# Plain products at the start of both half-step FFNs, in a hybrid decoder step on one core

## The chip, the cores and the metric

The kernel runs on one core of one Trainium2 chip. The time is device microseconds, the median of three runs. The engines are TensorE (PE, with its weight loads as PEld), VectorE (DVE), ScalarE (ACT), GpSimd (POOL) and SyncE (SP), whose queue issues all the DMAs.

## What is computed

512 prompt tokens and 8 sample tokens, 520 columns in all, go through one layer of width 1024, in fp32:

```python
def swiglu(x, w_gate, w_up, w_down):
    return (jax.nn.silu(x @ w_gate) * (x @ w_up)) @ w_down          # 1024 -> 2816 -> 1024

def layer(x, ...):
    x = x + 0.5 * swiglu(rmsnorm(x, norm_ffn1_w), ffn1_w_gate, ffn1_w_up, ffn1_w_down)
    mix, ... = token_mix(rmsnorm(x, norm_mix_w), ...)   # Mamba-2 scan, short conv, w_out
    x = x + mix
    x = x + 0.5 * swiglu(rmsnorm(x, norm_ffn2_w), ffn2_w_gate, ffn2_w_up, ffn2_w_down)
```

followed by a last RMSNorm. The outputs are the 520 rows and the new states.

## The kernel before

Everything lies transposed: features on the 128 partitions, the 520 tokens along the free axis, in two halves T0 and T1 of 260. x is four tiles `x0` to `x3` of two k-tiles each (a k-pair `e`).

Products of fp32 accuracy are made from three: an operand is split into `hi` (a cast on ACT, line 146) and `lo` (the rest, a subtraction on DVE, line 147), and PE adds hi·hi, hi·lo and lo·hi. The half of a weight split is `both`; `split` takes the next loaded item of the list `items`, splits one part of it into a pair of buffers of `whl` (four pairs) and, when the item is done, calls `load` for the next one (two raw buffers, one queue on SP). The order of the items is the order in which the kernel takes them, written out beforehand by `steps` and `ffn_items`.

A half step works on 11 pairs of hidden blocks. Each pair `p` has a gate (`G`) and an up (`U`) of 256 output features, and the down products (`D`) of earlier pairs are spread between them. Every gate or up is one `group` call: a product of 2 x 2 blocks by the seven-product scheme with shared sums (lines 218 to 241), so it needs sums of weight blocks (`adds`, lines 132 to 134, tile `S`) and sums of blocks of x. Its seven blocks are made of 12 matmuls each (four k-pairs, three products). The forms of x, called 0 to 6, are in `vbh`/`vbl` (three plain blocks, hi and lo) and `vth`/`vtl` (four sums), made by `variants` (lines 248 to 261) once for each k-pair, from x times the norm weight. `Gate` and `Up` evacuate the PSUM banks; the token's RMS factor `r` comes in there, and not into x, so the products don't wait for it. The pool `pst` has six banks.

At the start of the first half step, for each k-pair, x lands, `variants` makes its forms, and the squares go to two sums, on POOL (`square`) for the first two k-pairs and on ACT and POOL for the others. `factor` sums them over the partitions with a matmul by ones (line 286), and takes root and reciprocal (lines 287, 288). At the start of the second half step, the same forms are made by `nx2(d // 2)`, called after each pair of output features of the output projection in `mixer` (line 991 adds it to x). The pool for the weight sums, `c.sp`, is open within a half step alone; outside, `split` returns without doing anything on an item of kind "S".

In the mixer, the normed x is `Plain` (hi and lo, in the buffers of `vth`, `vtl`), the convolved channels `xs` lie six to a tile in the buffers of `vbh`, `vbl`, and the gated group's operands `gh`, `gl` (lines 980, 982) have tiles of their own. Instructions are put in order by a planner that goes by its own estimate of times; each engine then runs its queue in order.

## Time and profile before

| | us |
|---|---|
| median of three runs | 1185.29 (1183.92 to 1186.41) |
| the profiled execution, its own time | 1180.4 |
| its span, first to last instruction | 1178.6 |
| PE busy | 1117.5 (95%) |
| DVE busy | 897.8 (76%) |
| ACT busy | 523.5 (44%) |
| POOL busy | 227.1 (19%) |

All times of the trace are microseconds from the start of the span. In it, the first half step's matmuls run from 8.86 to about 391.6, the mixer's up to 799.6, the second half step's from 801.6. A busy PE isn't PE at its peak; the number of matmuls in a stretch tells more, since nearly all of them are 260 columns wide. The granted clock is a share of 2.4 GHz.

### The profile page before, as it was taken

Reading aid. Unit: us, or ns where it says so; the run is one execution under the profiler, and the core shown is the slowest. Engines: PE = TensorE matmul, PEld = TensorE weight load, DVE = VectorE, ACT = ScalarE, POOL = GpSimd, SP = SyncE. Lnnn points to the kernel's source line nnn. Section 1 sums busy time; section 2 is a strip of 40 time slices with the busy share of each in tenths; the row PEclk is TensorE's granted clock in tenths of the full one; section 3 lists DMA queues with packets and bytes.
Section 4 is the critical chain, followed back from the end, with each engine's and each line's share of the span. In section 5 each row is a group of like instructions: output and inputs, shape, how many; then the busy total and the mean of one; then the engine's idle time right before and its main releaser. Section 6 shows DMA issues by size and latency. Waiting matters only on the chain.

```text
span 1178.6 us, 21684 instructions
## 1 busy us (share of the span) xinstructions
PE 1117.5 (95%) x9059; PEld 1095.7 (93%) x9059; DVE 897.8 (76%) x1305; ACT 523.5 (44%) x750; POOL 227.1 (19%) x302
## 2 busy tenths in 40 slices
PE   4899999999999999998799999997999999999995
PEld 3799999999999999987799999997999999999994
DVE  8899777877766778889886677547988777786855
ACT  5555344444435576343322444323644444443442
POOL 5000000000002577566662232111000000000002
PEclk6899999999999999999799999998999999999998
DMA  5132332222333523455532322321332233322233
GB/s 182 36 108 77 113 131 81 81 85 98 110 100 103 157 83 118 141 171 171 177 126 79 95 73 95 103 90 36 108 103 98 75 103 108 112 99 101 78 95 73
DMA packets 45466, 122.97 MB, mean 104 GB/s; under 512 B 9336, under 2 KB 17432, under 8 KB 39864
## 3 DMA queue, kind: packets, MB, share of 16 engines
q1 hardware_dynamic: 45368, 121.58, 32.0%
q8 instruction: 71, 1.16, 0.4%
q14 instruction: 27, 0.22, 0.1%
HBM read 114.43 MB, written 7.14 MB: 103 GB/s over the span
## 4 chain that ended last, share of the span: by engine, by line
PE 79%; DVE 8%; POOL 5%; issue 3%; DMA 2%; ACT 2%; DVEq 0%; SPq 0%; POOLq 0%; ACTq 0%
PE pst L211 37%; PE auxt L522 21%; PE mmt L195 20%; DVE lo L147 2%; POOL up L891 1%; POOL st L892 1%; DVE r L288 1%; ACT hi L146 1%; DMA raw<-in_wu 1%; DMA out_ss<-st 1%; DMA st<-in_ssm 1%; DVE S L132 1%; DVE cv L766 1%; DVE vtl L261 0%; DVE y L604 0%
## 5 line engine op out<-in xcount | busy, mean ns | idle before, releaser
L146 ACT CAST hi<-raw 128x1024 fp32r<-128x1024 f32 (+2 forms) x212 | 185.8, 878 | 269.5 <-PE pst L211 86.3
L147 DVE TENSOR_TENSOR lo<-raw,hi 128x1024 fp32r<-128x1024 f32 (+2 forms) x212 | 220.3, 1040 | 50.0 <-ACT hi L146 47.3
L211 PE MATMUL pst<-vtl,hi 128*128 128x260 f32 x704 | 199.4, 284 | 6.8 <-DVE vtl L261 6.8
L211 PE MATMUL pst<-vth,hi 128*128 128x260 f32 x704 | 199.4, 285 | 4.2 <-ACT vth L260 3.5
L522 PE MATMUL auxt<-hh,hi 128*128 128x260 f32 x704 | 197.7, 283 | 1.1 <-DVE x L523 0.7
L522 PE MATMUL auxt<-hl,hi 128*128 128x260 f32 x704 | 197.6, 283 | 0.0
L211 PE MATMUL pst<-vth,lo 128*128 128x260 f32 x704 | 196.9, 284 | 0.2 <-DVE lo L147 0.2
L522 PE MATMUL auxt<-hh,lo 128*128 128x260 f32 x704 | 194.5, 283 | 0.0
L211 PE MATMUL pst<-vbh,hi 128*128 128x260 f32 x528 | 150.6, 289 | 10.7 <-ACT hi L146 5.1
L211 PE MATMUL pst<-vbl,hi 128*128 128x260 f32 x528 | 150.0, 287 | 5.1 <-DVE vbl L258 4.0
L195 PE MATMUL mmt<-vth,hi 128*128 128x260 f32 x704 | 146.5, 288 | 0.0
L211 PE MATMUL pst<-vbh,lo 128*128 128x260 f32 x528 | 145.1, 286 | 0.5 <-DVE lo L147 0.5
L195 PE MATMUL mmt<-vtl,hi 128*128 128x260 f32 x704 | 143.4, 284 | 0.0
L195 PE MATMUL mmt<-vth,lo 128*128 128x260 f32 x704 | 142.9, 285 | 0.0
L211 PEld LDWEIGHTS pst<-vtl,hi 128*128 128x128 f32 x704 | 133.5, 190 | 7.3 <-DVE vtl L261 7.3
L270 POOL TENSOR_TENSOR acc<-x 128x520 f32<-128x520 f32 x4 | 4.2, 1053 | 698.3 <-DVE x L523 678.0
L211 PEld LDWEIGHTS pst<-vth,hi 128*128 128x128 f32 x704 | 132.7, 189 | 6.4 <-ACT vth L260 4.2
L522 PEld LDWEIGHTS auxt<-hh,hi 128*128 128x128 f32 x704 | 132.2, 188 | 2.3 <-DVE x L523 1.1
L211 PEld LDWEIGHTS pst<-vth,lo 128*128 128x128 f32 x704 | 132.3, 190 | 0.8 <-DVE lo L147 0.8
L522 PEld LDWEIGHTS auxt<-hl,hi 128*128 128x128 f32 x704 | 132.5, 188 | 0.0
L522 PEld LDWEIGHTS auxt<-hh,lo 128*128 128x128 f32 x704 | 130.8, 188 | 0.0
L146 ACT CAST hi<-S 128x1024 fp32r<-128x1024 f32 x88 | 91.2, 1050 | 75.2 <-PE pst L211 53.2
(217 smaller groups left out, 2256.9 us busy)
## 6 DMA issues: line engine op xcount, KB each, us to landing
raw<-in_wi SPq DMA_DIRECT2D x45, 512.0 KB, 3.5
raw<-in_wu SPq DMA_DIRECT2D x22, 1024.0 KB, 4.9
raw<-in_wg SPq DMA_DIRECT2D x21, 1024.0 KB, 4.8
raw<-in_wd SPq DMA_DIRECT2D x48, 384.0 KB, 3.2
raw<-in_wo SPq DMA_DIRECT2D x16, 512.0 KB, 3.8
raw<-in_wd SPq DMA_DIRECT2D x16, 256.0 KB, 2.7
st<-in_ssm SPq DMA_DIRECT2D x16, 256.0 KB, 2.7
s<-scr SPq DMA_DIRECT2D x8, 512.0 KB, 4.6
```

The costliest lines, as they stand in the source:

```text
L132: V.tensor_tensor(s[:, 1:3], r[:, 0:4:2], r[:, 3:4].broadcast_to([P, 2, 512]), op=ALU.add)
L146: self.S.copy(hi, src)
L147: self.V.tensor_tensor(lo, src, hi.bitcast(F32), op=ALU.subtract)
L195: self.PE.matmul(ps[:, h, :H2], w[:, k, :], x[:, h * H2:(h + 1) * H2], start=first and n == 0, stop=last and n == 2)
L211: self.PE.matmul(ps[:, :H2], a[:, k, :], b, start=first and k + i == 0, stop=k == n - 1 and i == 2, skip_group_check=True)
L270: self.G.tensor_tensor(acc, xt, xt, op=ALU.mult)
L288: self.V.reciprocal(r[:, hs], r[:, hs])
L522: PE.matmul(ps[:, :H2], w[:, k, :], v, start=k + n == 0, stop=k == nk - 1 and n == 2)
L766: V.scalar_tensor_tensor(cv[:, :SEQ], raw[:, k:k + SEQ], w[k], cv[:, :SEQ], op0=ALU.mult, op1=ALU.add)
L891: G.tensor_tensor(up, bb, xd.unsqueeze(2).broadcast_to([P, HB, NS]), op=ALU.mult)
L892: G.tensor_tensor(st, st, up, op=ALU.add)
```

## The change

The first gates and ups of a half step (three in the first, two in the second: `LEAD`) are no longer grouped, but plain products: `pair` takes the two halves of the weights (kind "Q", no sums) and makes 2 output tiles x 2 token halves x 8 k-tiles x 3 matmuls, each output tile and half in a bank of its own.

The very first gate is written out: x is loaded by k-tile (the first one in two halves), and the gate's weights in four quarters, each between the k-tiles that need it; each k-tile's hi and lo parts and each quarter's are made as they land, and 12 matmuls follow for that k-tile into four banks. The squares of k-tiles 0 to 4 are POOL's, those of 5 to 7 ACT's, with the last two sums on DVE. The next two weights are loaded after x.

`Blocks` now keeps x's plain parts by k-tile (`xh`, `xl`, as `Plain` does), of which the grouped products' three plain blocks are slices; the four sums are made by `forms`, after the first gate and between the plain products, and no longer ahead of the start. In the second half step only the plain parts are made within the output projection.

Buffers move with it: four tiles of eight columns (`xh`, `xl`, `th`, `tl`) in place of four others; in the mixer the convolved channels take six columns each of `th` and `tl`, the sample step's B, C and update tiles and `rr` lie in their free columns, and `gh`, `gl` lie in `xh`, `xl`, where the mixer's x was.

```diff
+LEAD = {1: 3, 2: 2}
...
+        elif kind == "Q":
+            step = len(item) - 4
+            hi, lo = self.parts(None, (2, n * P))
+            self.both(r[:, 2 * step:2 * step + 2], hi, lo)
+            item.append(True)
+            self.ready.append((hi, lo))
+            if not step:
+                return
...
+    def pair_k(self, ps, w, m, k, x, first, last, hs=(0, 1)):
+        hi, lo = (t[:, k % 2 ^ m, k // 2 * P:(k // 2 + 1) * P] for t in w[m])
+        xh, xl = x
+        for h in hs:
+            for n, (a, b) in enumerate(((hi, xh), (hi, xl), (lo, xh))):
+                self.PE.matmul(ps[h][:, :H2], a, b[:, h * H2:(h + 1) * H2], start=first and n == 0, stop=last and n == 2)
+
+    def pair(self, x, bank, ev):
+        w = [self.take(), self.take()]
+        for m in range(2):
+            for h, ts in enumerate((T0, T1)):
+                ps = bank()
+                for k in range(KD):
+                    self.pair_k((ps, ps), w, m, k, x(k), k == 0, k == KD - 1, (h,))
+                ev.plain(m, ts, ps)
+            self.split()
+        ev.whole()
...
-    def variants(self, src, bh, bl, th, tl):
+    def forms(self, src, th, tl):
...
-        S.copy(bh[:, 0], src[:, 0, T0])
-        S.copy(bh[:, 1:].rearrange("p v n -> p (v n)"), src[:, 1])
...
-        V.tensor_tensor(bl[:, 0], src[:, 0, T0], bh[:, 0].bitcast(F32), op=ALU.subtract)
-        V.tensor_tensor(f(bl[:, 1:]), src[:, 1], f(bh[:, 1:]).bitcast(F32), op=ALU.subtract)
...
+    def parts(self, d, ts):
         c = self.c
...
+        w = c.par(self.wname, d)
+        xt, hi, lo = self.x[d // 2][:, d % 2, ts], self.xh[:, d, ts], self.xl[:, d, ts]
+        c.S.activation(hi, xt, AF.Copy, scale=w)
+        c.V.scalar_tensor_tensor(lo, xt, w, hi.bitcast(F32), op0=ALU.mult, op1=ALU.subtract)
...
+class Blocks(Plain):
+
+
+    def forms(self, e):
...
+        xw = c.tv.tile([P, 2, T], F32, tag="xw", name="xw")
         for m in range(2):
...
+            c.S.activation(xw[:, m], self.x[e][:, m], AF.Copy, scale=c.par(self.wname, 2 * e + m))
+        c.forms(xw, self.th[:, e], self.tl[:, e])
...
+    def plain(self, m, ts, ps):
+        self.c.V.tensor_tensor(self.dst[:, m, ts], ps[:, :H2], self.r[:, ts], op=ALU.mult)
...
-    for e in range(NQ):
-        for m in range(2):
-            nc.sync.dma_start(x[e][:, m], a["xT"][2 * e + m])
-        if e == 0:
-            c.load(pieces=2)
-    c.load()
...
-            if start:
-                for e in range(NQ):
-                    nx.operands(e)
-                    if e == 0:
-                        c.adds()
-                        c.split()
-                    for m in range(2):
-                        if e < 2:
-                            c.square(acc[0], x[e][:, m], e + m == 0)
-                        elif e + m == 2:
-                            S.activation(acc[1], x[e][:, m], AF.Square)
-                        else:
-                            c.square(acc[1], x[e][:, m], False, True)
...
+                raw = c.raw.tile([P, 4 * 512], F32, tag="raw", name="raw").rearrange("p (b m) -> p b m", b=4)
+                w0 = [c.parts(None, (2, 512)) for _ in range(2)]
+                ps = [(bank(), bank()) for _ in range(2)]
+                for k in range(KD):
+                    e, m = divmod(k, 2)
+                    for i, hs in enumerate((T0, T1) if k == 0 else (slice(0, T),)):
+                        nc.sync.dma_start(x[e][:, m, hs], a["xT"][k][:, hs])
+                        nx.parts(k, hs)
+                        if m == 0 and i == 0:
+                            q = slice(e * P, (e + 1) * P)
+                            nc.sync.dma_start(raw[:, :, q], a["wg1"][0][:, :, q])
+                            for j, (hi, lo) in enumerate(w0):
+                                c.both(raw[:, 2 * j:2 * j + 2, q], hi[:, :, q], lo[:, :, q])
+                    for j in range(2):
+                        c.pair_k(ps[j], w0, j, k, nx.of(k), k == 0, k == KD - 1)
+                    if k < 5:
+                        c.square(acc[0], x[e][:, m], k == 0)
+                    elif k == 5:
+                        S.activation(acc[1], x[e][:, m], AF.Square)
+                    else:
+                        sq = c.tv.tile([P, T], F32, tag="t4", name="sq2")
+                        S.activation(sq, x[e][:, m], AF.Square)
+                        V.tensor_tensor(acc[1], acc[1], sq, op=ALU.add)
+                c.load()
+                c.load()
                 c.prime()
                 r = c.factor(acc, D)
+                ev = Gate(c, fp, g, r)
+                for j in range(2):
+                    for h, ts in enumerate((T0, T1)):
+                        ev.plain(j, ts, ps[j][h])
+                ev.whole()
+                nx.forms(0)
+                nx.forms(1)
+                later = [2, 3]
             else:
                 c.prime()
                 r = nx.factor()
+                later = list(range(NQ))
...
+                if kind != "D":
+                    if kind == "G" and i[0]:
+                        while later:
+                            nx.forms(later.pop(0))
...
+                    if 2 * i[0] + (kind == "U") < LEAD[n]:
+                        c.pair(nx.of, bank, ev)
+                    else:
+                        c.group(NQ, B, bank, ev)
                 if kind == "G":
...
+                    while len(later) > 2:
+                        nx.forms(later.pop(0))
...
+        xst = [c.vp.tile([P, KD, T], F32, tag=n, name="xs") for n in ("th", "tl")]
+        rr = xst[1][:, 7]
+        place = [t[:, :SEQ].rearrange("p (b n) -> p b n", n=NS) for t in (xst[0][:, 6], xst[0][:, 7], xst[1][:, 6])]
...
-                    hi = yp.tile([P, T], F32R, tag=f"gh{j}", name=f"gh{j}")
...
+                    if j == 0:
+                        gh, gl = (c.vp.tile([P, KD, T], F32R, tag=n, name="g" + n) for n in ("xh", "xl"))
```

## Rows read from the trace of the kernel before

**Rows 1.** The page, part 1: busy us, share of the span, instructions.

```profile
PE 1117.5 (95%) x9059; PEld 1095.7 (93%) x9059; DVE 897.8 (76%) x1305; ACT 523.5 (44%) x750; POOL 227.1 (19%) x302
```

**Rows 2.** Busy time by stretch (stretch, its length, engines, clock, DMA share, GB/s).

```profile
core 0: us, PE busy (x) PEld busy (x) DVE busy (x) ACT busy (x) POOL busy (x), PEclk, DMA share, GB/s
9.00:20.00 11.00, 4.27 (x13) 2.77 (x13) 11.00 (x9) 5.34 (x8) 8.53 (x5) 0.50 0.50 201
40.00:60.00 20.00, 18.86 (x150) 18.17 (x149) 14.98 (x19) 10.52 (x15) 0.00 (x0) 1.00 0.15 54
60.00:80.00 20.00, 20.00 (x167) 19.92 (x166) 19.35 (x28) 12.00 (x17) 0.00 (x0) 1.00 0.31 106
...
200.00:260.00 60.00, 60.00 (x500) 59.79 (x499) 46.56 (x69) 25.14 (x34) 0.00 (x0) 1.00 0.31 105
...
760.00:820.00 60.00, 52.86 (x415) 51.47 (x414) 35.08 (x37) 19.60 (x29) 6.12 (x4) 0.94 0.21 71
820.00:840.00 20.00, 20.00 (x167) 19.85 (x167) 17.32 (x26) 11.93 (x18) 0.00 (x0) 1.00 0.29 106
```

**Rows 3.** The same by stretch for line 211, the grouped products' matmuls, alone.

```profile
0.00:20.00 20.00, 4.41 (x13) 2.91 (x13) 0.72 0.62 216
20.00:40.00 20.00, 9.13 (x29) 6.73 (x30) 0.59 0.15 52
40.00:60.00 20.00, 18.86 (x150) 18.17 (x149) 1.00 0.15 54
```

**Rows 4.** PE's waits (total us, times, longest), 0 to 60, then 760 to 830.

```profile
PE pst L211 <- DVE vbl L258: 4.0, 1, 4.0
...
PE pst L211 <- DVE vtl L261: 4.5, 1, 4.5
PE pst L211 <- DVE x L991: 1.8, 1, 1.8
```

**Rows 5.** Timeline of POOL and DVE at the start (start, us, instruction, wait before it).

```profile
4.00 1.05 POOL L270 TENSOR_TENSOR acc<-x 128x520 f32<-128x520 f32 x1 [3.57 <-DMA x<-in_xT]
...
9.84 1.54 POOL L276 TENSOR_TENSOR sq<-x 128x520 f32<-128x520 f32 x1 [2.09 <-DMA x<-in_xT]
...
11.45 2.15 POOL L277 TENSOR_TENSOR acc<-acc,sq 128x520 f32<-128x520 f32 x1
...
12.38 2.32 DVE L261 TENSOR_TENSOR vtl<-t,vth 128x1040 fp32r<-128x1040 f32 x1
...
35.20 1.17 DVE L261 TENSOR_TENSOR vtl<-t,vth 128x1040 fp32r<-128x1040 f32 x1
```

**Rows 6.** Timeline of PE, two matmuls in a row.

```profile
39.23 0.42 PE L211 MATMUL pst<-vth,hi 128*128 128x260 f32 x1
...
39.45 0.39 PE L211 MATMUL pst<-vtl,hi 128*128 128x260 f32 x1
```

**Rows 7.** Groups of DVE by line and shape, whole span: busy, mean ns | idle before.

```profile
L147 DVE TENSOR_TENSOR lo<-S,hi 128x1024 fp32r<-128x1024 f32 x88 | 106.7, 1220 | 16.6 <-ACT hi L146 16.5
...
L380 DVE TENSOR_TENSOR g<-cp,pst 128x260 f32<-128x260 f32 x66 | 27.8, 421 | 10.5 <-PE pst L211 6.8 <-ACT cp L366 2.9
...
L405 DVE TENSOR_TENSOR g<-g,r 128x1040 f32<-128x1040 f32 x22 | 27.2, 1237 | 2.7 <-ACT g L404 2.7
...
L288 DVE RECIPROCAL r<-r 128x260 f32<-128x260 f32 x10 | 17.2, 1750 | 2.5 <-ACT r L287 2.5
...
L403 DVE TENSOR_TENSOR g<-g,r 128x520 f32<-128x520 f32 x22 | 15.3, 695 | 0.2
...
L315 DVE SCALAR_TENSOR_TENSOR vtl<-x,pc,vth 128x520 fp32r<-128x520 f32 x8 | 6.0, 756 | 0.6 <-ACT vth L314 0.6
```

**Rows 8.** Timeline: last z product's evacuation, first gated operand's matmuls, later row sums.

```profile
707.09 0.68 DVE L962 TENSOR_TENSOR z<-mmt,r 128x520 f32<-128x520 f32 x1
...
719.00 0.40 PE L195 MATMUL mmt<-gh,hi 128*128 128x260 f32 x2
...
804.61 1.14 PE L286 MATMUL auxt<-acc,ones 128*128 128x260 f32 x4
```

**Rows 9.** Group of POOL by line and shape: the sample step's updates.

```profile
L891 POOL TENSOR_TENSOR up<-bb,xd 128x512 f32<-128x512 f32 x16 | 25.5, 1593 | 28.4 <-DVE ys L896 28.3
```

More of the change, by code (lines that the diff above doesn't have):

```diff
@@ L344, in __call__, with factor, of @@
             self.acc = c.new_acc()
-        self.operands(e)
+        for d in (2 * e, 2 * e + 1):
+            self.parts(d, slice(0, T))
+            c.square(self.acc, self.x[e][:, d % 2], d == 0, True)
+    def factor(self):
+        return self.c.factor([self.acc], D)
+    def of(self, k):
+        return self.xh[:, k], self.xl[:, k]
+class Blocks(Plain):
+    def forms(self, e):
+        c = self.c
+        if e == 0:
+            self.th, self.tl = (c.vp.tile([P, NQ, 4, H2], F32R, tag=n, name="f" + n) for n in self.tags[2:])
+        xw = c.tv.tile([P, 2, T], F32, tag="xw", name="xw")
         for m in range(2):
-            c.square(self.acc, self.x[e][:, m], e + m == 0, True)
+            c.S.activation(xw[:, m], self.x[e][:, m], AF.Copy, scale=c.par(self.wname, 2 * e + m))
+        c.forms(xw, self.th[:, e], self.tl[:, e])
     def __getitem__(self, vk):
         v, k = vk
-        return (self.bh[:, k, v], self.bl[:, k, v]) if v < 3 else (self.th[:, k, v - 3], self.tl[:, k, v - 3])
-    def factor(self):
-        return self.c.factor([self.acc], D)
+        if v < 3:
+            d, ts = ((0, T0), (1, T0), (1, T1))[v]
+            return self.xh[:, 2 * k + d, ts], self.xl[:, 2 * k + d, ts]
+        return self.th[:, k, v - 3], self.tl[:, k, v - 3]
 class Evac:
@@ L419, in c12, with plain, whole @@
         c.V.tensor_tensor(h[:, 1], h[:, 1], g[:, 1], op=ALU.mult)
+    def plain(self, m, ts, ps):
+        self.c.V.tensor_tensor(self.dst[:, m, ts], ps[:, :H2], self.g[:, m, ts], op=ALU.mult)
+    def whole(self):
+        pass
 def steps(n):
@@ L479, in build, with ffn @@
     acc = [c.new_acc(), c.new_acc()]
-    for e in range(NQ):
-        for m in range(2):
-            nc.sync.dma_start(x[e][:, m], a["xT"][2 * e + m])
-        if e == 0:
-            c.load(pieces=2)
-    c.load()
-    def ffn(nx, start, after, halves_last=None):
+    def ffn(n, nx, after, halves_last=None):
         with ExitStack() as c2:
@@ L495, in ffn @@
             bank = lambda: pp.tile([P, 512], F32, tag="ps", name="pst")
[L496 to L508 removed]
+            g = fp.tile([P, 2, T], F32, tag="g", name="g")
@@ L573, in last @@
         if e == 0:
-            ys.append(c.vp.tile([P, KD, T], F32, tag="vth", name="y"))
+            ys.append(c.vp.tile([P, KD, T], F32, tag="th", name="y"))
             ys.append(c.new_acc())
@@ L586, in last_half @@
         PE.matmul(ps[:, :H2], c.ones, facc[:, hs], start=True, stop=False)
-        sq = c.vp.tile([P, 2, H2], F32, tag="vbl" if h else "vbh", name="sq")
+        sq = c.vp.tile([P, KD, T], F32, tag="xl" if h else "xh", name="sq")[:, :2, :H2]
         S.activation(sq, x[e][:, :, hs], AF.Square)
@@ L607, in last_half @@
                 nc.sync.dma_start(o["yT"][:, e0:e1, ts], y[:, e0:e1, ts])
-    ffn(nx2, False, last, last_half)
+    ffn(2, nx2, last, last_half)
 def mixer(c, o, x, nxt, nx2):
@@ L753, in mixer @@
         xs = [None] * NX
-        xst = [c.vp.tile([P, 6, T], F32, tag=n, name="xs") for n in ("vbh", "vbl")]
         def conv(i):
@@ L870, in sample @@
             HB = NB // 2
-            bcs = sd.tile([P, HB, NS], F32, tag="up", name="bcs")[:NB]
+            bcs = place[2][:NB]
             V.tensor_copy(bcs.rearrange("b t n -> b (t n)"), pbc[:NB])
@@ L877, in sample @@
                     bs = slice(k * HB, (k + 1) * HB)
-                    bb = sd.tile([P, HB, NS], F32, tag="bb", name="bb")
-                    cc = sd.tile([P, HB, NS], F32, tag="cc", name="cc")
+                    bb = place[0]
+                    cc = place[1]
                     nc.sync.dma_start(bb, scb[g, bs].unsqueeze(0).broadcast_to([P, HB, NS]))
@@ L889, in sample @@
                             S.activation(st[:, b], st[:, b], AF.Copy, scale=ddc[:, j, 1, k * HB + b:k * HB + b + 1])
-                        up = sd.tile([P, HB, NS], F32, tag="up", name="up")
+                        up = place[2]
                         G.tensor_tensor(up, bb, xd.unsqueeze(2).broadcast_to([P, HB, NS]), op=ALU.mult)
```

70 lines of the change are left out of this document (24 added, 46 removed).

## The prediction

> **What bounds the kernel now.** I read the page's first part, then a table of busy time by stretch. The page says that TensorE (PE) is at work nearly all the time [rows 1]. The table says where it is not: in a stretch from the middle of the first half step PE is busy for the whole 60 us and issues 500 matmuls, 0.12 us each, while the stretches ahead of 60 us and the one that holds the second half step's start fall short of that [rows 2]. So the kernel is PE's matmul count times 0.12 us, plus what PE loses at a few places, and the change touches two of them.
>
> Start of the first half step: PE has issued only 192 of that half step's matmuls by 60.0 us [rows 3]. At 0.12 us they are 23.0 us, so 37 us were lost. PE's waits name the forms of x one after another, VectorE's (DVE's) vbl and vtl among them [rows 4]. DVE is busy through the whole of 9 to 20 us in spite of only nine instructions [rows 2]: the timeline shows why [rows 5]. A DVE instruction that took 1.17 us alone took 2.32 us with a GpSimd (POOL) one beside it, and a POOL one that took 1.05 us alone took 2.15. In that stretch the two engines take turns. Third, the granted clock is at the low level (0.50, 1.2 GHz) there, and matmuls start 0.22 us apart [rows 6].
>
> Start of the second half step: 760 to 820 us holds 415 matmuls where 500 would fit, 85 x 0.12 = 10.2 us lost, and 820 to 840 is full again [rows 2]. The waits are 4.5 us for vtl of the last k-pair and 1.8 us for the last x [rows 4]; the clock fell with them.
>
> **The change, part by part.** Durations of DVE by size [rows 7]: 128x260 0.42, 128x520 0.70, 128x520 with a scalar 0.76, 128x1024 1.22, 128x1040 1.24, a reciprocal of 128x260 1.75.
>
> *More matmuls.* A grouped gate or up is 7 blocks x 4 k-pairs x 3 = 84 matmuls; a plain one is 2 x 2 x 8 k-tiles x 3 = 96. Three in the first half step add 36, 4.3 us; two in the second add 24, 2.9 us. All on the path.
>
> *The first gate, k-tile by k-tile.* It needs of DVE, ahead of each k-tile, the low part of x (0.76; the first k-tile in two halves, 0.84) and, every other k-tile, two low parts of a weight quarter (128x256, 0.42 each by the nearest size). Through k-tile 3 this is 0.84 + 0.84 + 0.76 + 0.76 + 0.84 + 0.76 = 4.8 us. POOL squares five k-tiles with nine instructions. If the two engines take turns as they do there [rows 5], k-tile 3 is ready after 4.8 us of DVE and eight POOL instructions of 1.05: from the 4.0 us at which the first x had landed [rows 5], 4.0 + 4.8 + 8.4 = 17.2. K-tile 2 is ready one x part and one POOL turn or so earlier, at about 15.6. A k-tile is 12 matmuls: 2.6 us at the low level, 1.44 at the high one. I take two of them from 15.6 at the low level and the last four at the high one, since PE then has a queue of ready matmuls, as from 40 us on, where the clock is at 1.00 [rows 2]: 15.6 + 5.2 + 5.8 = 26.6. The DVE side of the last k-tile ends at 4.0 + 9.5 (POOL) + 10.2 (17 low parts and one sum of squares) = 23.7, so it does not set the end. Bounds: 20 if POOL costs DVE nothing, 31 if the clock stays low. Landing isn't the limit: the third x k-tile landed at 9.84 behind 1 MB of weights [rows 5], and here 0.25 MB stand ahead of it. On SP's queue 13 issues replace 10, and the next weights go behind them; the second of these loads waits there for the first gate's buffer, till its last low part at about 22, with nothing queued behind that the first gate needs, and nothing of the two is due before the first gate ends.
>
> *What stays ahead of the comparison point.* Before has 2904 - 192 = 2712 matmuls of the half step left at 60.0 us. After has 2940, so it has as many left after 228: the first gate's 96 and 132 more, 15.8 us. The four matmuls with the ones matrix for the row sums take 1.1 us [rows 8]. The gate's four banks of six come free only when the factor is there: last square about 24, row sums, two reciprocals (3.5 us), first evacuation, about 33; the first up needs its third bank 48 matmuls in, at 27.7 + 5.8 = 33.5. I put 0.5 us on it (0 to 2).
>
> *The forms of x made meanwhile.* Four calls of 0.70 + 2 x 0.42 + 1.24 = 2.8 us of DVE, 11.1 in all, now beside the plain products. First grouped product is the second up; its third block is the first to read a form, at 27.7 + 23.0 + 2.9 = 53.6. DVE has from 23.7 until then 29.9 us, and these are ahead: a sum 0.7, reciprocals 3.5, first gate's evacuation 4 x 0.42 + 1.24 = 2.9, low parts of the first up 2.4, forms 11.1, the first up's evacuation 1.7, second gate's low parts 2.4 and evacuation 1.7, the sums for the second up's weights 1.22 + 2 x 0.7 = 2.6, its first two low parts 2.4: 31.4 us. Two more of 1.24 each, the low part of h and the gate's last product, may go ahead: 33.9. So PE waits 1.5 to 4; I take 2.5 (0 if the queue order is lucky, 6 if forms come last). Dropping vbl (1.1 us of DVE per k-pair) is in this list by absence; ScalarE has room (5.34 of 11 us in the first of these stretches [rows 2]).
>
> First half step: 26.6 + 1.1 + 15.8 + 0.5 + 2.5 = 46.5 against 60.0: 13.5 us gained.
>
> *Second half step.* x's parts are two instructions per k-tile instead of the whole set, made inside the output projection, so at its end only the last evacuation (0.70), a ScalarE copy and a 0.76 us low part stand between x and its k-tile, which PE reaches after 21 matmuls (2.5 us): 0.4 us of wait. The plain weights need no sums, and so are split ahead of this start; the grouped ones couldn't be, as their pool was not open. Of the 10.2 us lost, the row sums' 1.1 stay, 0.4 too, 2.9 go to the added matmuls. For the forms the same list: due 27.4 us after the projection's end, against 0.7 + 0.76 + 1.2 + 3.5 + 2.9 + 11.1 + 1.7 + 1.24 + 2.6 + 2.4 = 28.1 of DVE, with some idle at its start: again 2.5 (0 to 6). Gain 10.2 - 1.1 - 0.4 - 2.9 - 2.5 = 3.3.
>
> *Mixer.* The gated part's operands now live where the mixer's x lay, and so are written only after the last z product: eight low parts of 0.76, 6 us, between the last z at 707.09 and their first matmul at 719.00 [rows 8]. They fit: 0 (0 to 3). The other renamed places (rr, B, C and the update in free columns) add no instruction: 0, but see the second rival.
>
> Sum: 13.5 + 3.3 = 16.8 us. The profiled execution took 1180.4 (span 1178.6); it would take 1163.6. The median of the runs is 1185.3, 4.9 above; I take the difference of 16.8 over to it and predict 1168.5.
>
> **Rivals.** *Forms late.* If both waits for forms are at their upper end, 6 us, the time is 1168.5 + 7 = 1175.5. For it: DVE is at 19.35 of 20 us in 60 to 80 us even now [rows 2]. Against: plain weights take two low parts and no sums, where grouped ones take four low parts and 2.6 us of sums. Chance 0.20.
>
> *Low clock through the first gate.* PE waits for each k-tile, the clock stays at the low level, and the gate ends at 31: 1168.5 + 4.4 = 1173. The clock is at 1.2 GHz through the stretch in which PE waits between matmuls [rows 2, 6], which speaks for it; that k-tiles 3 to 7 come about 1.6 us apart, (23.7 - 17.2) / 4, faster than PE eats them at that level (2.6), speaks against. The Trainium skill ("TensorE: Matmul & The Clock Gate", section "HAM oscillation — how this bites in real kernels") describes a kernel in which each k-tile's work was shorter than the wait for the next, so that the clock fell anew at every one; by that rule the time is this rival's. The trace agrees that the low level goes with waits. Chance 0.12.
>
> *Renamed places serialise the mixer.* B, C and the update tile now share two tiles with the convolved channels. If waits went by tile and not by column, the sample step's 16 rounds would wait for the scan's instructions and hold them back; POOL already waits 28.4 us in those rounds [rows 9], and as much again on PE's path gives 1168.5 + 28 = 1197, slower. It decides from 16.8 / 16, about 1 us a round. Against: the channels shared tiles before too, and no such wait shows. Chance 0.06.
>
> *No earlier start.* If the planner orders PE so that the first gate's matmuls wait as the grouped ones did, the first half step gains nothing and pays 4.3: 1185.3 + 4.3 - 3.3 = 1186. Chance 0.05.
>
> **How the numbers follow.** Forecast 1168.5, chance 0.57. Its bounds: gate at 20 and no waits for forms, 6.6 + 0.5 + 5 = 12 less, 1156; the upper ends of all, 1180. Together these corners are unlikely, so 8 in 10 is 1158 to 1178, which takes in the first two rivals. A measurement tells 0.2%, 2.4 us, from no change. Faster: 0.57 + 0.20 + 0.12 = 0.89, less 0.01 for the corners, 0.88; same 0.05 (most of the fourth rival, and a corner); slower 0.07.
>
> **What would show it.** First matmuls of the first gate about 6 us instead of 8.86, its last about 27; DVE and POOL lengthened beside each other until about 18; about 228 half-step matmuls issued by 46 us; 415 matmuls in the 60 us around the second start becoming about 475; a wait of PE on vtl's successor of 1.5 to 4 us at the first grouped product of each half step; the mixer's length unchanged. If the mixer changes by more than 3 us, or PE waits at the plain products for weights, the sum is wrong.

## The result, and the profile after

The changed kernel takes 1173.19 us (median of four runs, 1166.82 to 1176.91) against 1185.17 for the kernel before in the same comparison (1183.92 to 1186.41): ratio 0.9893, interval 0.9848 to 0.9938. It is faster by 12 us where 16.8 were forecast, and the forecast's 1168.5 is 4.7 us too low.

The profiled execution of the changed kernel took 1172.36, its span is 1170.6. Busy time, share and instructions, from the first part of its page, beside [rows 1]:

```profile
PE 1123.9 (96%) x9119; PEld 1101.7 (94%) x9119; DVE 871.6 (74%) x1279; ACT 514.4 (44%) x731; POOL 224.6 (19%) x301
```

PE issues exactly 60 matmuls more than before (9119 against 9059): the 36 and 24 of the sum. Then the table of busy time by stretch, which answers [rows 2] (stretch, its length, the engines, granted clock, DMA share, GB/s):

```profile
9.00:20.00 11.00, 9.12 (x54) 8.18 (x52) 10.65 (x10) 6.46 (x14) 9.59 (x7) 1.00 0.61 221
...
40.00:60.00 20.00, 19.31 (x155) 18.57 (x154) 19.00 (x30) 11.42 (x14) 0.00 (x0) 1.00 0.16 54
60.00:80.00 20.00, 18.15 (x140) 17.20 (x141) 16.06 (x23) 9.53 (x15) 0.00 (x0) 1.00 0.15 53
760.00:820.00 60.00, 58.72 (x486) 58.41 (x485) 37.76 (x44) 22.53 (x28) 7.48 (x4) 1.00 0.24 85
820.00:840.00 20.00, 15.40 (x106) 13.11 (x105) 15.38 (x22) 10.54 (x16) 0.00 (x0) 1.00 0.13 47
```

Three things are to be seen. The start works: PE issues 54 matmuls in 9 to 20 where it issued 13, at a clock of 1.00 where it had 0.50. There is a hole that was not there, from the end of 40 to 60 (155 where 167 fit) into 60 to 80 (140, where before had 167). And the hole of the second start has not gone, it has moved: 760 to 820 now lacks 14 of 500 instead of 85, but 820 to 840, which was full, lacks 61 of 167. 61 x 0.12 = 7.3 us.

The plain products' matmuls alone (line 256) up to 46.5 us, the moment that the forecast named, answer [rows 3]; the grouped products have issued none by then:

```profile
0.00:46.50 46.50, 35.98 (x257) 34.27 (x258) 1.00 0.48 161
```

PE's largest waits, first two of 0 to 60 and then three of 760 to 830 (total us, times, longest), beside [rows 4]:

```profile
PE pst L256 <- DVE lo L149: 1.7, 3, 0.7
PE pst L256 <- DVE g L427: 1.3, 1, 1.3
...
PE pst L221 <- DVE lo L149: 1.4, 2, 1.0
PE pst L256 <- DVE x L1053: 1.3, 1, 1.3
PE pst L221 <- DVE fxl L286: 0.8, 1, 0.8
```

No single wait is long any more: 1.3 us at most. In the holes PE goes on with other blocks for as long as it has some, and waits in many small pieces; there the count of matmuls in a stretch says more than the list of waits.

To place gains and losses I cut each execution at two instructions: the start of the first half step's last down matmul, and the start of the last evacuation of the mixer's output projection. For the kernel after they are the last times of these two lines (count, shortest/median/longest ns, first to last start):

```profile
L576 PE MATMUL auxt<-hh,lo x43: 278/282/283, 360.0 to 378.2; 128*128 128x260 f32 x43
...
L1053 DVE TENSOR_TENSOR x<-mmt,x x8: 686/699/700, 722.9 to 790.8; 128x520 f32<-128x520 f32 x8
```

Cut so, in us, one profiled execution in each row, with the experiments in the order in which they are told below:

| kernel | first half step ends | mixer | second half step | span |
|---|---|---|---|---|
| before | 391.4 | 409.4 | 377.8 | 1178.6 |
| before, again | 391.9 | 411.1 | 379.7 | 1182.7 |
| after | 378.2 | 412.6 | 379.8 | 1170.6 |
| after, again | 379.1 | 411.7 | 379.9 | 1170.7 |
| forms first in both half steps | 385.4 | 407.5 | 372.2 | 1165.1 |
| three plain products in the second | 378.9 | 409.7 | 375.8 | 1164.4 |
| own buffer for xw | 381.6 | 407.2 | 378.0 | 1166.8 |
| own buffer, forms first in both | 380.0 | 410.3 | 371.6 | 1161.9 |
| forms first in the second only | 379.6 | 416.7 | 372.8 | 1169.1 |
| the same, again | 378.6 | 411.5 | 372.1 | 1162.2 |
| own buffer, forms first in the second | 381.6 | 410.8 | 371.8 | 1164.2 |
| no squares on POOL | 372.3 | 414.2 | 380.7 | 1167.2 |
| squares on ACT | 381.5 | 413.0 | 372.3 | 1166.8 |
| one plain product fewer in each | 387.7 | 412.6 | 382.3 | 1182.6 |

By the means of the two executions of either kernel, the first half step gained 13.0 us (forecast 13.5), the second lost 1.1 (forecast a gain of 3.3), and the mixer is 1.9 longer (forecast 0): 10.0 in all. The medians differ by 12.0; single executions of the changed kernel lie up to 10 us apart, and where two profiles of one kernel differ by 6.9 us (forms first in the second only, below), 5.2 of it lie in the mixer. Most of what follows is on the second half step, which is 4.4 us off its forecast.

### The profile page after: what moved, and what is told of

It is laid out like the page before. It is cut to its first block, busy times and chain, and to the rows that moved or that the text cites. A ratio compares the mean times of both kernels' runs of the same rounds, so it can differ in the third digit from the quotient of the medians.

```text
span 1170.6 us, 21766 instructions
## 1 busy us (share of the span) xinstructions
PE 1123.9 (96%) x9119; PEld 1101.7 (94%) x9119; DVE 871.6 (74%) x1279; ACT 514.4 (44%) x731; POOL 224.6 (19%) x301
## 4 chain that ended last, share of the span: by engine, by line
PE 80%; DVE 6%; POOL 4%; issue 3%; DMA 3%; ACT 3%; SPq 0%; DVEq 0%; POOLq 0%; ACTq 0%
PE pst L221 32%; PE mmt L205 21%; PE auxt L576 20%; PE pst L256 3%; DVE lo L149 2%; POOL xs L955 1%; POOL st L956 1%; ACT hi L148 1%; DMA st<-in_ssm 1%; DMA raw<-in_wu 1%; DMA out_ss<-st 1%; PE auxt L904 0%; DVE y L666 0%; DVE xxl L339 0%; POOL ce L871 0%
## 5 line engine op out<-in xcount | busy, mean ns | idle before, releaser
L148 ACT CAST hi<-raw 128x1024 fp32r<-128x1024 f32 (+3 forms) x218 | 188.5, 869 | 292.8 <-PE mmt L205 105.7
L149 DVE TENSOR_TENSOR lo<-raw,hi 128x1024 fp32r<-128x1024 f32 (+3 forms) x218 | 227.0, 1044 | 60.5 <-ACT hi L148 57.6
L205 PE MATMUL mmt<-xxh,hi 128*128 128x260 f32 x704 | 146.5, 289 | 0.0
L205 PE MATMUL mmt<-xxl,hi 128*128 128x260 f32 x704 | 143.8, 285 | 0.0
L205 PE MATMUL mmt<-xxh,lo 128*128 128x260 f32 x704 | 143.6, 286 | 0.0
L205 PEld LDWEIGHTS mmt<-xxh,hi 128*128 128x128 f32 x704 | 110.2, 190 | 0.6
L205 PEld LDWEIGHTS mmt<-xxl,hi 128*128 128x128 f32 x704 | 110.0, 190 | 0.3 <-issue 0.2
L205 PEld LDWEIGHTS mmt<-xxh,lo 128*128 128x128 f32 x704 | 110.0, 191 | 0.1
L149 DVE TENSOR_TENSOR lo<-S,hi 128x1024 fp32r<-128x1024 f32 x78 | 94.4, 1218 | 19.6 <-ACT hi L148 19.3
L221 PE MATMUL pst<-fxh,hi 128*128 128x260 f32 x320 | 90.7, 286 | 0.8 <-ACT hi L148 0.4
```

Source lines behind the costliest of these rows:

```text
L148: self.S.copy(hi, src)
L149: self.V.tensor_tensor(lo, src, hi.bitcast(F32), op=ALU.subtract)
L205: self.PE.matmul(ps[:, h, :H2], w[:, k, :], x[:, h * H2:(h + 1) * H2], start=first and n == 0, stop=last and n == 2)
L221: self.PE.matmul(ps[:, :H2], a[:, k, :], b, start=first and k + i == 0, stop=k == n - 1 and i == 2, skip_group_check=True)
```

## Experiments

Theory A: the loss behind the plain products is a matter of buffers. A form's call scales x into `xw`, and `xw` has the same single buffer as `h`, the up's result; so the calls for k-pairs 2 and 3 can't begin before `h` of the first up has been read. Theory B, the prediction's: DVE has too much to do by the time the forms are due. Theory C came out of the runs: it is the place of the calls in the program. The change calls the forms of pairs 2 and 3 behind the first up.

**The changed kernel again.**

> The changed kernel once more, unaltered, for a second profile and more runs. In its first profile the first half step gained 13.3 us (its matmuls end at 378.3 instead of 391.6), the mixer took 3.3 us more (412.5 us from there to the last sum of the output projection, before 409.2), and the second half step 1.6 us more (380.4 instead of 378.8 us from the projection's last matmul to the end). If the mixer's 3.3 us come from the new order and places, they are here again, 412 to 413; if they are a matter of one execution, the mixer takes 408 to 414 and differs from the first profile by more than 1 us. Time: 1167 to 1177 either way.

1173.27 us (1171.64 to 1174.14), ratio 0.9911 (0.9896 to 0.9926). The mixer's 411.7 lies just outside the 412 to 413 of the one case and within 1 us of the first profile, which the other excluded, so it decides nothing. The second half step is again 379.9, and 55 to 75 us again holds 128 matmuls: both holes are the kernel's, not one execution's.

**All forms ahead of the first up.**

```diff
-                later = [2, 3]
+                nx.forms(2)
+                nx.forms(3)
+                later = []
...
-                    while len(later) > 2:
+                    while later:
```

> All four calls for the forms of x stand ahead of the first up instead of two ahead of it and two behind. Theory A, a buffer: the scratch tile xw, of which there is one, also holds the first up's result h, so that the last two calls wait until h's low part is made (their first instruction stands at 46.34 and 819.53 us, right behind it). Then the last form's low part ends about 10 us earlier in both half steps (before 50 and before 818), PE's lost matmuls at 55 to 75 us (38, 4.6 us) and at 820 to 840 (61, 7.3 us) mostly come back: 7 to 11 us faster than the changed kernel, about 1163. Theory B, DVE's load, as predicted: DVE has more to do ahead of the first grouped product than fits, and the order doesn't matter much: the wait moves to the first up, within 2 us of the changed kernel.

1169.96 us (1166.84 to 1172.82), ratio 0.9884 (0.9862 to 0.9906), between what the two theories gave. The small total hides two large parts: the second half step is 7.6 us shorter than after's, its hole is gone, and the first is 7.2 us longer. PE's longest wait between 25 and 60 us says why:

```profile
PE pst L256 <- DVE h L449: 7.6, 1, 7.6
```

The first up has no bank left because its result can't be written: `h` waits for the buffer, which now the last two calls' `xw` hold. So the shared buffer is a price, but a price of this order, not of the changed kernel's.

**Three plain products in the second half step too.**

```diff
-LEAD = {1: 3, 2: 2}
+LEAD = {1: 3, 2: 3}
```

> Three plain products instead of two in the second half step: the second gate is plain there too. It adds 12 matmuls, 1.4 us. The first grouped product comes 11.5 us of PE later, so that forms that end at about 830 us would be there in time. Theory A and B both give the 7.3 us lost at 820 to 840 back for 1.4: 5 to 6 us faster than the changed kernel, 1167. If the loss there isn't from the forms but from the weights' buffers (of four pairs, freed only as PE goes on), it stays, and the time is 1 to 2 us longer than the changed kernel's.

1168.46 us (1166.23 to 1170.92), ratio 0.9879 (0.9861 to 0.9897). Twelve more matmuls, 1.4 us, and yet the second half step is 4.0 us shorter. What PE lost there was waiting for forms, and plain work fills it. Both theories had expected 5 to 6 us less in all, and the medians differ by 4.7; the rival, by which the loss stays, is refuted.

**A buffer of its own for xw**, out of the ring that holds `hh`; the order of the program stays. (A buffer of its own for `h` instead, the first idea, has no room: its pool would need 40.625 KB per partition where 36.75 are left, so there is no time for it.)

```diff
+            fw = [hp.tile([P, 2, T], F32, tag="hh", name="xw") for _ in range(NQ)]
...
-        xw = c.tv.tile([P, 2, T], F32, tag="xw", name="xw")
```

> The scaled x of the forms (xw) gets a buffer out of the ring of hh tiles instead of the one buffer that it shares with the up's result h. Program order, planner and all instructions stay those of the changed kernel; the forms of pairs 2 and 3 still stand behind the first up. Theory A (the shared buffer holds the forms): the ACT copies of xw no longer wait for hl of the first up; the last low part of the forms ends some 5 to 8 us earlier than 60.5 and 828.8, the stretches 55 to 75 and 820 to 840 get back most of their 4.6 and 7.3 us, and the time falls by 7 to 11 us from the changed kernel's 1173, to 1162 to 1166. Theory B (VectorE's load holds them, as the prediction had it): the copies are earlier, but the subtractions end where they did, and the time stays within 2 us of 1173. A third case: the order that the planner gives VectorE, with the up's evacuations ahead of the forms, holds them, in which case only part comes back (2 to 5 us).

1174.2 us (1168.56 to 1175.78), ratio 0.9893 (0.9864 to 0.9923): the median did not move. Theory A falls. The second half step gained 1.8 us, the first lost 3.4. ACT's timeline (start, us, instruction, the wait before it) shows what still holds the forms, first in the kernel after, then in this one:

```profile
809.86 1.05 ACT L148 CAST hi<-S 128x1024 fp32r<-128x1024 f32 x1 [2.33 <-PE pst L256]
815.68 0.62 ACT L148 CAST hi<-raw 128x512 fp32r<-128x512 f32 x1 [4.77 <-PE pst L256]
816.21 1.06 ACT L609 CAST hh<-h 128x1040 fp32r<-128x1040 f32 x1
...
819.53 1.34 ACT L366 ACTIVATE xw<-x,pc 128x520 f32<-128x520 f32 x2
```

```profile
813.79 0.62 ACT L148 CAST hi<-raw 128x512 fp32r<-128x512 f32 x1 [4.77 <-PE pst L256]
814.32 1.07 ACT L610 CAST hh<-h 128x1040 fp32r<-128x1040 f32 x1
815.30 2.58 ACT L365 ACTIVATE xw<-x,pc 128x520 f32<-128x520 f32 x4
```

x had been there since the projection's end, about 790, and with the ring the buffers were free. But ACT stood still for 4.77 us before a weight cast that waits for the plain up's matmuls to let go of a weight buffer, and the scaling of x stands behind that cast and behind the cast of `h`. With the ring all four scalings run in one go (x4). Counted from the last evacuation's start they begin after 26.5 us instead of 28.7, and that is about what the buffer gives: 1.8 us.

**Own buffer, and all forms first.** Both edits together.

> As the run before, and the forms of all four pairs stand right behind the first gate in both half steps, ahead of the first up's evacuation. With the forms' order alone (the run forms_first) the first half step lost 7.3 us because the first up's result could not be written before the forms had let go of the shared buffer. Theory A: with a buffer of their own that loss is gone but for the up's evacuations standing behind more VectorE work (0 to 2 us); the second half step keeps the 7.6 us it gained; in all 1161 to 1165. Theory B (VectorE's load): the first half step is still about 7 us longer than in the changed kernel, since the subtractions ahead of the evacuation are the same; 1168 to 1171.

1164.75 us (1163.11 to 1165.94), ratio 0.9821 (0.9802 to 0.984). The second half step is 371.6, and 55 to 75 us holds 165 matmuls: both holes are gone. The same stretch in after and in this kernel (PE, clock, DMA share, GB/s):

```profile
55.00:75.00 20.00, 17.46 (x128) 1.00 0.20 74
```

```profile
55.00:75.00 20.00, 19.76 (x165) 1.00 0.25 81
```

The first half step still ends no earlier than after's, for another reason:

```profile
PE pst L256 <- DVE g L426: 5.2, 1, 5.2
```

That is the wait for banks ahead of the first gate's evacuation, 1.3 us in after. In this execution the first reciprocal begins at 30.64 and the first evacuation at 36.18 (26.84 and 32.43 in after). From the one to the other it is 5.5 and 5.6 us, so what is late is the reciprocal, by 3.8 us. ACT had waited 4.85 us for a load, and the last row sums, for which the root waits, come later on PE's queue, in after and in this kernel:

```profile
24.45 1.92 PE L311 MATMUL auxt<-acc,ones 128*128 128x260 f32 x8
```

```profile
29.03 1.04 PE L311 MATMUL auxt<-acc,ones 128*128 128x260 f32 x4
```

This is not one execution's: the run with one plain product fewer (below), which has the same start, has its last row sums at 29.44, ACT's wait for a load at 5.01 and the wait for banks at 4.9. With the buffers free, ACT also scales x between the first gate's k-tiles (11.00 busy of 9 to 20, against 6.46 in after). Which of these makes the factor late no run tells apart. Theory B's 7 us are not there.

**Forms first in the second half step only**, buffers as in the changed kernel; run twice.

```diff
-                    while len(later) > 2:
+                    while len(later) > (2 if n == 1 else 0):
```

> Buffers as in the changed kernel; the forms of pairs 2 and 3 stand ahead of the first up in the second half step alone, the first half step is untouched. If the two half steps' losses are independent, the second half step is some 7 us shorter (372 against 379.8) and the first stays at 378 to 379: 1164 to 1167. If the gain of forms_first in its second half step came from something that its slower first half step set up (other chance of the clock, DMA phase), it isn't seen here: 1172 to 1174.

1167.39 us (1164.48 to 1170.92), ratio 0.9836 (0.9813 to 0.9859): the two half steps are as the first case had them (379.6 and 372.8, a little over on the first), the median is 0.4 above its range.

> The run second_first once more, beside the run before on the same chip: which of the two is the better, and whether its long mixer (416.7 us from the first half step's last matmul to the last evacuation of the output projection, with the clock at 0.61 behind the wait at the mixer's start) was that execution's. If chance: first half step 378 to 380, second 372 to 373 again, mixer 407 to 413, profile 1160 to 1166, median 1165 to 1168. If the order of the second half step had a hand in the mixer: 415 to 418 again, profile 1168 to 1171.

1163.99 us (1161.57 to 1165.49), ratio 0.9815 (0.9786 to 0.9845). The second half step took 372.8 and 372.1, both times 7 us or more less than after, by order alone. This is theory C. The first run's long mixer, 416.7, was that execution's: the second has 411.5. The same stretches by 5 us (columns as above), kernel after and then the second run of this one:

```profile
805.00:810.00 5.00, 5.00 (x44) 5.00 (x43) 3.02 (x5) 2.64 (x4) 0.00 (x0) 1.00 0.01 3
...
815.00:820.00 5.00, 5.00 (x43) 5.00 (x43) 3.65 (x7) 3.33 (x5) 0.00 (x0) 1.00 0.36 123
820.00:825.00 5.00, 3.75 (x28) 3.12 (x26) 3.69 (x5) 3.31 (x6) 0.00 (x0) 1.00 0.21 87
825.00:830.00 5.00, 2.93 (x16) 2.11 (x16) 3.83 (x5) 1.87 (x2) 0.00 (x0) 1.00 0.01 2
```

```profile
805.00:810.00 5.00, 5.00 (x44) 5.00 (x43) 4.19 (x7) 4.85 (x6) 0.00 (x0) 1.00 0.01 3
...
815.00:820.00 5.00, 5.00 (x44) 5.00 (x43) 5.00 (x9) 2.99 (x5) 0.00 (x0) 1.00 0.16 26
820.00:825.00 5.00, 5.00 (x43) 5.00 (x43) 2.82 (x4) 2.10 (x4) 0.00 (x0) 1.00 0.45 188
```

In after DVE is idle for 1.98 of 805 to 810 and 1.35 of 815 to 820, while PE is about to run dry for want of DVE's results. In the other kernel it is idle for 0.81 and 0, and PE stays full. The groups of the forms' low parts tell the same (count, ns, first to last start):

```profile
L286 DVE TENSOR_TENSOR fxl<-t,fxh x4: 1234/1242/1242, 792.5 to 828.8; 128x1040 fp32r<-128x1040 f32 x4
```

```profile
L286 DVE TENSOR_TENSOR fxl<-t,fxh x4: 1228/1232/1241, 791.8 to 816.4; 128x1040 fp32r<-128x1040 f32 x4
```

From the last evacuation's start (790.8 and 790.1) the last form ends after 39.2 us in the one and 27.5 us in the other. With the forms first this is near the 28.1 us of the forecast's list of DVE's work; in the changed kernel's order it is not. The nearness is in part luck: DVE is busy for 25.4 of the 27.5 us, the low part of `h` that the list holds comes only behind, and x's last low part takes 1.80 us where the list has 0.76.

**Own buffer, forms first in the second half step only.**

> xw in a buffer of its own, the first half step's forms in the changed kernel's order (pairs 2 and 3 behind the first up), the second half step's all ahead of the first up. Theory (the order counts, the buffer only where forms go ahead of the up): the first half step ends where the changed kernel's does, 378 to 379.6, and the 381.65 of the run xw_ring was the low clock of that execution; the second half step takes 371.5 to 373; median 1164 to 1167. Rival (the buffer of its own lets forms 2 and 3 in ahead of work that is due earlier, as xw_ring's 381.65 may say): the first half step ends at 381 to 382 again, and the median is 1166 to 1169.

1165.83 us (1164.68 to 1166.34), ratio 0.9832 (0.9804 to 0.986). By the first half step the rival holds: it ends at 381.6 again, as in the first run with the buffer (the median itself lies in the theory's range). 55 to 75 us, here and in that first run (columns as in the last such rows):

```profile
55.00:75.00 20.00, 16.06 (x97) 0.83 0.15 55
```

```profile
55.00:75.00 20.00, 16.04 (x97) 0.83 0.16 59
```

97 matmuls both times, 128 in after. What I had called one execution's low clock comes with this kernel. With the buffer free, DVE's instructions fall into another order: in the earlier of these two runs the second form's low part starts at 49.8 instead of 43.3 and the last at 62.6 instead of 60.5, and PE waits 2.6 us for low parts of weights (L149). Which of these brings the clock down the runs leave open.

**No squares on POOL at the start.** The squares of k-tiles 1 to 4 and their sums are left out, so the first norm's factor lacks these terms.

```diff
-                    if k < 5:
-                        c.square(acc[0], x[e][:, m], k == 0)
+                    if k == 0:
+                        c.square(acc[0], x[e][:, m], True)
+                    elif k < 5:
+                        pass
```

> GpSimd's squares of k-tiles 1 to 4 and their sums are left out at the start (the first norm's factor then lacks these four terms, so the values after it differ). Theory: GpSimd and VectorE lengthen each other while both work on SBUF, and that paces the first gate's k-tiles; without the squares VectorE's casts of 9 to 20 us go at their later speed and the first gate's last matmul ends at 20 to 22 us instead of 24.5, and the whole is 2 to 4 us shorter. Rival: the loads pace the k-tiles; the gate ends within 0.5 us of 24.5 and the whole is unchanged.

The first half step ends at 372.3, 5.9 us earlier than after's, and the one time is 1169.01. The gate's last matmul starts at 20.57 instead of 24.34, as the theory had it. DVE's timeline in the kernel after and in this one:

```profile
13.45 3.26 DVE L339 SCALAR_TENSOR_TENSOR xxl<-x,pc,xxh 128x520 fp32r<-128x520 f32 x2
16.64 2.71 DVE L149 TENSOR_TENSOR lo<-raw,hi 128x256 fp32r<-128x256 f32 x2
```

```profile
11.08 1.43 DVE L339 SCALAR_TENSOR_TENSOR xxl<-x,pc,xxh 128x520 fp32r<-128x520 f32 x2
12.42 0.75 DVE L149 TENSOR_TENSOR lo<-raw,hi 128x256 fp32r<-128x256 f32 x2
```

Two low parts of weights take 2.71 us beside POOL's squares and 0.75 without them. The Trainium skill ("SBUF — State Buffer", section "SBUF: two separate sides") says that a VectorE instruction with two operands in SBUF and a GpSimd one that reads SBUF exclude each other for a whole instruction; the trace agrees, as far as these lengthened times (2.71 against 0.75) can show it.

**Squares on ACT instead**, on top of own buffer and forms first.

```diff
-                        c.square(acc[0], x[e][:, m], k == 0)
+                        c.square(acc[0], x[e][:, m], k == 0, True)
```

> The run xw_ring_first (own buffer for xw, all forms right behind the first gate), and beside that the squares of k-tiles 1 to 4 are taken by ScalarE instead of GpSimd, which is left with the sums of them: about half of GpSimd's work at the start. Nothing is left out. Theory (GpSimd and VectorE take turns, and that paces the first gate): half of what leaving out the squares gave in the first half step, about 3 of 6 us; the gate's matmuls end at about 22 to 23 us and the median falls from 1164.75 to 1161 to 1163. Rival: ScalarE, which the changed kernel's trace has busy for 6.00 of the 6 us from 9 to 15, becomes the pace with four more squares of 0.62 us; no gain or a loss of up to 2 us, 1164 to 1167.

1165.32 us (1162.73 to 1168.57), ratio 0.983 (0.9809 to 0.9852): no gain over 1164.75; the rival holds. 9 to 20 us, and POOL's sums with their waits:

```profile
9.00:20.00 11.00, 9.54 (x72) 8.67 (x72) 7.94 (x13) 11.00 (x22) 2.47 (x2) 1.00 0.61 222
```

```profile
20.79 1.31 POOL L302 TENSOR_TENSOR acc<-acc,sq 128x520 f32<-128x520 f32 x1 [5.21 <-ACT sq L299]
23.74 1.77 POOL L302 TENSOR_TENSOR acc<-acc,sq 128x520 f32<-128x520 f32 x1 [1.64 <-ACT sq L299]
```

DVE has room (7.94 of 11 us), PE issues 72 matmuls (54 in after, 56 in the run that it starts from). But ACT is busy for all 11, as it was in that run even without these squares (11.00), the sums come late, and the wait for the first gate's banks is 7.0 us instead of 5.2. What the gate gained the factor gave back.

**One plain product fewer in each half step**, on top of own buffer and forms first.

```diff
-LEAD = {1: 3, 2: 2}
+LEAD = {1: 2, 2: 1}
```

> The run xw_ring_first with one plain product fewer in each half step: gate and up in the first, the gate alone in the second. This shows what the plain products cover. In xw_ring_first the last forms were there at 61.3 and 818.3, and the first grouped product began at about 54 and 815.4. Theory (the forms' chain of some 5 us a pair sets when grouped products can run, and the plain products only hide it): each half step saves 12 matmuls, 1.4 us, and waits longer for the forms, by 5 to 10 us in the first and 2 to 8 us in the second; in all 5 to 15 us slower than xw_ring_first, profile 1167 to 1177. Rival (the planner has enough other blocks, or the forms come as much earlier as they are needed earlier): 1 to 3 us faster than xw_ring_first.

1184.5 us, span 1182.6: 20.7 us longer than the run that it starts from, slower than either theory said. The first half step lost 7.7 and the second 10.7; the rest, 2.3, lies in the mixer. The cover of two plain products, 192 matmuls or 23 us, is worth many times the added matmuls.

**The kernel before again.**

> The kernel before once more, for a second profile of its mixer. In the changed kernel and its variants the stretch from the first half step's last matmul to the start of the second half step's work took from 407 to 417 us, where the one profile of before has 409.2; the clock had fallen behind the wait at the mixer's start in four of eight. If the change has a hand in it (the mixer's loads come later against a first half step that ends 13 us earlier), before has its wait there at 1.4 to 1.6 us again, the clock at 1.00 behind it, and 407 to 410 us. If it is chance alone, before may show 411 to 414 and the low clock as well. One more profile can refute the first, not prove it.

1184.52 us: mixer 411.1, clock 1.00 behind the wait, and the wait itself 1.7 us. So before alone spans 409.4 to 411.1, and the twelve executions with the changed mixer 407.2 to 416.7, mean 411.5 against 410.3. That is no difference these runs can tell; neither expectation is refuted. One part of it may go with the change. PE's wait at the mixer's start, in before and in after:

```profile
PE auxt L684 <- ACT tbl L296: 1.5, 1, 1.5
```

```profile
PE auxt L749 <- ACT tbl L321: 1.9, 1, 1.9
```

Behind it stands a load: ACT's cast ahead of the norm's factor waits 0.6 us for a weight load in before, 1.0 in after, and 2.0 in the run without squares, where PE waits 2.9. PE's wait is 1.5 and 1.7 us in the two executions of before and 1.4 to 2.9, mean 2.1, in the twelve with the changed mixer; ten of these are above 1.7. It is 1.9 to 2.9 in the six in which the first half step ends at 379.6 or earlier, but 2.3 and 2.4 at 381.6 and 381.5 as well. So some 0.5 us may be given back there; that the earlier end of the first half step does it is not shown.

## Why the prediction was right or wrong

*Added matmuls: right.* 60, as counted.

*First gate: right in its mechanism, 2.0 us too long.* The first matmul starts at 5.39 (about 6 was expected), the last ends at 24.34 + 0.28 = 24.6 where 26.6 was forecast, with the turns of DVE and POOL that [rows 5] showed. I let two k-tiles run at the low clock, 2 x (2.6 - 1.44) = 2.3 us; here it was at 1.00 throughout, and in the eleven other executions of the changed kernel and its variants between 0.84 and 1.00 over 9 to 20 us (1.00 in six). So the rival of the low clock did not come about. It drew on the Trainium skill ("TensorE: Matmul & The Clock Gate", section "HAM oscillation — how this bites in real kernels"), whose kernel has each k-tile's work shorter than the wait for the next. That is not so in this trace, which thus neither bears the page out nor speaks against it: a k-tile's 12 matmuls are 1.44 us, and PE's longest single wait in the gate was 0.7. The run without squares shows that the turns set the pace: 3.8 us of the gate. (The 0.22 us between matmuls that I put to 9 to 20 us I had read at 39 us [rows 6].)

*Bank wait: 0.5 forecast, 1.3 measured*, within its bounds.

*Forms in the first half step: 2.5 forecast, 4.7 measured.* 257 matmuls were out by 46.5 us instead of 228, since the wait was not yet paid: 29 x 0.12 = 3.5 us ahead. Then 55 to 75 us held 128 instead of 167: 39 x 0.12 = 4.7. That it is the forms' place and buffer is seen from the runs in which this stretch is full (165 matmuls, above), not from a wait: no single long one is there, as the forecast had expected. The gate's 2.0 too long and the forms' 2.2 too short nearly cancel and leave 13.0 beside the 13.5. The sum was right in part by that luck, and the total does not vouch for its terms.

*Second half step: wrong, and this is the step that failed.* "For the forms the same list ... again 2.5 (0 to 6)". I had summed DVE's work and put it against the due time as if DVE could do it in any order. The sum itself was near, in part by luck: 27.5 us when the forms stand first. What failed is that in this program they stand behind the first up, on ACT's queue behind casts that wait for weight buffers (4.77 us at a stretch), so that DVE had idle time and the forms came 39.2 us in. The price was 7.3 us, outside the bounds of 0 to 6. The 0.4 us for x, put behind 21 matmuls, was 1.3 and stood elsewhere: PE waits for the last evacuation (L1053, above) ahead of its very first plain matmul, as it had for 1.8 us before. 10.2 us had been lost before; now it is (14 + 61) x 0.12 = 9.0, and the added matmuls cost 2.9: 10.2 - 9.0 - 2.9 = -1.7, beside the loss of 1.1 (means) or 2.0 (the two first executions) in the table. The check that I had named was too narrow: 760 to 820 us was to hold about 475 matmuls and holds 486, and the loss stood behind it. Forms first turn it into a gain of 378.75 - 372.45 = 6.3 (means of two executions each), twice what I forecast: with them in the second run PE's only wait from 788 to 845 us is those 1.3, so the forms cost 0 instead of 2.5, and 3.3 + 2.5 = 5.8 is near the 6.3. In the rival "forms late" I had the right place and the wrong cause: I argued it from DVE's load, and the run that changes nothing but the order leaves that load as it is.

*The same mechanism in the first half step* is shown only in part. With a buffer of its own for xw both orders cost about the same there (381.6 and 380.0). Forms late, PE runs dry at 55 to 75; forms first, the factor comes late and PE runs dry at 30 to 40 (28 matmuls, 73 in after). No run that leaves nothing out got both at once, and what makes the factor late is open.

*Mixer: 0 forecast; not to be told from 0* by these runs (1.9 by the means). By the first two profiles alone it grew by 3.2 us, more than the 3 that I had named as a sign of a wrong sum; the second profile of either kernel takes that back. The wait at its start is longer in most. The rival of the renamed places (28 us) is refuted by every row of the table, and so is that of no earlier start.

*The number.* By the medians 4.7 us off. By the profiles it is 16.8 - 10.0 = 6.8: 0.5 in the first half step, 4.4 in the second, 1.9 in the mixer. The 2 us between the two ways of counting no run explains.

The best versions are forms first in the second half step alone, 0.9836 and 0.9815 in its two runs, and own buffer with forms first in both, 0.9821. Their intervals overlap; both have lower medians than the changed kernel (0.9893 and 0.9911), and the first has them by one condition in one line.

## What to carry to other kernels

A list of what an engine must do before a due time is a lower bound. Before trusting it, look at what stands ahead of that work on each engine's queue, and what that in turn waits for: work whose inputs have long been there, placed behind an instruction that waits for a buffer, waits with it. When PE has other blocks to run, a loss no longer shows as one long wait but as fewer matmuls in a stretch, so count them. And test a shared buffer and an order separately: here the buffer looked guilty in the trace, and freeing it alone moved no median; only with the forms first did it count.

## What the runs showed of the hardware that I had not expected

The clock fell behind PE's wait at the mixer's start in six of the twelve executions with the changed mixer and not in the others, at waits of about the same length: 8 us from 394.31 of after had 0.79, while the second run with the forms first in the second half step only, after a wait of 2.2 us against after's 1.9, had 1.00 (PE, clock, DMA share, GB/s):

```profile
394.31:402.31 8.00, 8.00 (x56) 0.79 0.19 68
```

```profile
394.31:402.31 8.00, 8.00 (x69) 1.00 0.21 68
```

At 1.00 such a stretch holds 69 matmuls, so this cost 13 x 0.12 = 1.6 us; in the execution with the longest mixer it was 46 matmuls at 0.61, 2.8 us.

At the first gate it is much the same. The run without squares had 0.88 over 9 to 20 us, after 1.00. The low level (1.2 GHz) lies at the start of that stretch, behind waits of PE between 5 and 8 us, of which either kernel has some (PE busy for 2.07 of these 3 us in after, 1.94 without squares). 8 to 12 us, in after and in the run without squares:

```profile
8.00:12.00 4.00, 4.00 (x20) 1.00 1.06 352
```

```profile
8.00:12.00 4.00, 4.00 (x20) 0.57 1.07 360
```

Both issue 20 matmuls there, so beside after the low clock lost none; whether the run without squares would have issued more at 1.00 is open. From 12 to 20 us both have 1.00.
